# A hybrid decoder layer on one core: smaller groups for z, another product order, conv means two tiles sooner, all low weights on VectorE

## The chip, the core and the metric

The kernel runs on one core of a Trainium2 chip. A core has a matrix engine (TensorE, PE in the profile; its weight loads are PEld), VectorE (DVE), ScalarE (ACT), GpSimd (POOL) and SyncE (SP), which here issues most of the DMA transfers. The metric is the device time of one launch in microseconds (us). Three runs of the kernel before took 1290.45, 1290.51 and 1292.22 us.

## The reference

One layer of a decoder, for 1024 tokens of width 1024, with 16 meta tokens put in front (1040 rows). All is in 32-bit floats.

- `h` is the layer norm of the input. `z = h @ w_in + b_in` is cut into queries (512 columns), keys (128), values (128), the input of a convolution branch (2 x 512) and gates (2 x 1024).
- Attention branch: 8 query heads on 2 key heads of width 64, a window of 128 positions in blocks of 128, 16 meta keys that are always seen, a relative bias and a sink in the softmax. Its output is projected to width 1024.
- Convolution branch: `c = value * sigmoid(gate)`, a causal depthwise convolution over 31 taps, a layer norm over the 512 channels, `silu`, a projection to width 1024.
- `mixed = sigmoid(g_A) * A + sigmoid(g_B) * B`, then `h = LN(alpha * h + mixed @ w_out)`.
- A feed-forward part: up to 2 x 2816 columns, a causal depthwise convolution over 3 taps, `gelu(g) * u`, down to 1024, and a last layer norm.

## The kernel before

**Products.** Activations are kept transposed: channels on the partitions, rows (tokens) along the free axis. A tile of 128 output channels is one set of weights, 8 blocks of 128 x 128 for a depth of 1024. To keep the precision of 32-bit floats, each operand is split into a high half, rounded to TensorE's 32-bit format, and a low half, the rest. `product` (lines 334, 337 and 338) then issues three matmuls for each block: high weights by high activations, high by low, low by high. So each weight tile needs `split` (line 300: ScalarE copies and rounds the high half; line 303: the low half by a subtraction, on VectorE if `quick`, else on POOL). `weights` counts the tiles; the first thirty are quick, and the last eight of them, those of the two projections, are not. `prep_wo` splits the eight weight tiles of the output product with the same function: the first four on VectorE, the last four on POOL.

**z.** `z_tile` takes one weight tile through a list of groups of columns; each group is accumulated over 8 blocks x 3 matmuls into one bank of PSUM (tag "mm", three banks) and evicted. HG, the list for the convolution tiles, has 272, 384 and 384 columns; TG, the list for queries and gates, is the same without the first 14 rows (258, 384, 384). There are 27 such tiles: 8 of the convolution (`conv_chunk`, a gate tile and a value tile for each of four chunks), 3 of queries and 16 of gates (`gate_tile`; line 716 evicts a gate through a Tanh on ScalarE, and the result is stored to DRAM as `sgd`). The first products of z (line 540) run earlier, while the input is still being normalised.

**Order.** The program is written in one sequence with priorities (`rank`, `tc.cur_priority`); a scheduler orders each engine's instructions by them when the kernel is built, and the engines run their queues in that order. `after` adds an edge for that scheduler alone. Attention (lines 780 to 900) has a higher priority than the gate tiles, and the 124 operations of the 31 taps of four chunks (lines 707 and 709, VectorE) a lower one, so gate tiles fill TensorE and taps fill VectorE between the steps of attention. A step there is: scores (lines 870 and 871, TensorE), bias and maximum (line 874, VectorE), exponentials (line 886, ScalarE), transposes (line 894), splits of the weights (line 897 ScalarE, line 898 VectorE) and the product with the values.

**The norm of the convolution branch.** `csum` adds the four chunks (POOL twice, then VectorE, line 925). The means (line 930) are products of `csum` with a matrix of 1/512, held back until gate tile 12. Then come, for three groups of columns (UG: 386, 384, 256), the centring (line 968), squares and their sum (974 to 980), the inverse root with a refinement step (985 to 989: one table function on ScalarE, four operations on VectorE), the scaling and Silu (996, 997), and the split (1003, 1004). ScalarE's functions lie in tables; the profile shows an ACT_TABLE_LOAD where another table is needed. VectorE's operations there are pinned in the written order. `o_split` (1015 to 1017) divides attention's output by the softmax sums and splits it. These are the operands of the two projections (`ps_p`), eight weight tiles in groups PG of 258 and 3 x 256 columns.

**The feed-forward part.** The up-projection (`prod`, line 1509) is done in seven products in place of eight, on sums of halves: for each of 22 pairs of output chunks, seven products of 24 matmuls each, 12 on 258 and 12 on 256 columns. The seven operands of both halves of the rows lie where B_AT says, in the buffers RHC, RHO, OA, RX and OC. The weights come from a ring (RING) which takes over the buffers of the earlier weight tiles. The down-projection is line 1634.

**Places.** High and low halves of a weight tile are two buffers, "whi" and "wlo", of 8 blocks of 144 columns each, of which 128 are used. W_FLAT = 96 is where a flat row of 1024 begins in one of them.

Of the kernel before, what the change touches and what calls it, by code (L numbers as in the profile page):

```python
# [29 lines left out]
P = 128  # L30
# [22 lines left out]
HG = [(0, 272), (272, 656), (656, 1040)]  # L53
UG = [(0, 386), (386, 770), (770, 1026)]
# [15 lines left out]
W_FLAT = 96  # L70
# [40 lines left out]
def tile_hybrid_layer(  # L111
# [187 lines left out]
    def split(raw, hi, lo, quick=False, behind=None):  # L299
        ins = nc.scalar.copy(hi, raw)  # L300
        if behind is not None:
            after(ins, behind)
        return (nc.vector if quick else nc.gpsimd).tensor_tensor(lo, raw, f32(hi), OP.subtract)  # L303
# [26 lines left out]
    def product(ps, terms, behind=None):  # L330

        n = len(terms)
        for i, (ah, al, bh, bl) in enumerate(terms):
            ins = nc.tensor.matmul(ps, ah, bh, start=i == 0, stop=False)  # L334
            if i == 0 and behind is not None:
                after(ins, behind)
            nc.tensor.matmul(ps, ah, bl, start=False, stop=False)  # L337
            last = nc.tensor.matmul(ps, al, bh, start=False, stop=i == n - 1)  # L338
# [16 lines left out]

    TG = [(a + U0 if i == 0 else a, b) for i, (a, b) in enumerate(HG)]

# [168 lines left out]
    def z_first(g, tiles, *ks, raw=False):  # L526
# [5 lines left out]
        for k in ks:  # L532
            for i in tiles:
# [5 lines left out]
                for j, (w, hl) in enumerate(((hi, 0), (hi, 1), (lo, 0))):  # L539
# [122 lines left out]
    ones = ones_of(cp)  # L662
# [22 lines left out]
    def conv_chunk(c):  # L685
# [8 lines left out]
        z_tile(in_cols(10 + c), HG, g_evac, wt_c1 if c == 1 else None)  # L694
# [7 lines left out]
        z_tile(in_cols(6 + c), HG, v_evac2)  # L702
        with rank(RK_CONV + c * 100):
            for j in range(TAPS):
                wc = cdw[:, j * CH + c:j * CH + c + 1]
                if j == 0:
                    nc.vector.tensor_scalar(acc[c], cin[:, j:j + U], wc, cdwb(c), OP.mult, OP.add)
                else:
# [1079 lines left out]
```

## Time and profile before

| what | value |
|---|---|
| median of three runs | 1290.51 us |
| the profiled execution, its own time | 1288.89 us |
| its span, first to last instruction | 1287.0 us |
| mean granted TensorE clock | 0.994 |
| TensorE busy | 1263.6 us |
| VectorE busy | 1083.7 us |
| ScalarE busy | 582.9 us |
| POOL busy | 49.8 us |

A rough course of the time, from the windows and the timeline: to 60 us the input norm and the first products of z, from then to 433 us the tiles of z with attention and the taps between them, to 520 us the two projections, to 631 us the output product and its norm, from about 639 to 1068 us the up-projection, then the down-projection and the last norm.

How to read the rows: times are in us from the first instruction. A row of the timeline has the start, the length, the engine, the line, the operation, the output and input by their names, the shape and a count; brackets behind it give the time that the engine had idled before it and what released it. The length of a matmul includes its way through the array, so consecutive matmuls overlap; the pace is the distance between their starts. A row of a group ends in busy time and mean length (us, ns), and then the idle time before its instructions and what ended it. A row of the windows has the window and its length, then busy time and count for each engine, the granted clock, the share of DMA time and GB/s. A row of the chain of waits has the start, the length, the engine, the output and the line.

### The profile page before, as it was taken

The numbers are of one execution on the slowest core, as the hardware profiler recorded it, in microseconds if no ns is written. First come the engines' busy times: TensorE is split into PE (matmuls) and PEld (weight loads), VectorE is DVE, ScalarE is ACT, GpSimd is POOL, SyncE is SP. The second block draws the span as 40 slices with busy tenths as digits, with TensorE's granted clock in tenths as the row PEclk, the third lists the DMA queues.
The fourth block names the chain that finished last, engine by engine and source line by source line (L and its number), as shares of the span: only waits on it lengthen the run. The fifth ranks groups of instructions, "written<-read, shape, count | busy, mean of one in ns | idle before, by whom it ended". The sixth has DMA issues, their size and how long they took to land.

```text
span 1287.0 us, 21685 instructions
## 1 busy us (share of the span) xinstructions
PE 1263.6 (98%) x8546; PEld 1191.0 (93%) x8546; DVE 1083.7 (84%) x1843; ACT 582.9 (45%) x1053; POOL 49.8 (4%) x28
## 2 busy tenths in 40 slices
PE   8999999999999999999999999999999999999997
PEld 7899999999999999788899999999999997888886
DVE  7889999999936987647899999989889886887697
ACT  5423334545547232244664554455545543535330
POOL 2100000010000132100000000000000000000000
PEclk8999999999999999999999999999999999999999
DMA  6265633333252665222235554453454566989722
GB/s 246 83 241 165 163 108 98 89 99 107 76 150 64 188 189 143 89 82 90 76 117 196 184 202 177 180 210 130 161 187 187 189 209 244 393 291 381 254 76 82
DMA packets 96296, 212.10 MB, mean 165 GB/s; under 512 B 11059, under 2 KB 36211, under 8 KB 95938
## 3 DMA queue, kind: packets, MB, share of 16 engines
q1 hardware_dynamic: 84426, 199.64, 46.3%
q10 hardware_dynamic: 11768, 11.08, 2.7%
q8 instruction: 67, 1.10, 0.4%
q14 instruction: 35, 0.29, 0.1%
HBM read 150.29 MB, written 62.70 MB: 165 GB/s over the span
## 4 chain that ended last, share of the span: by engine, by line
PE 88%; DVE 6%; DMA 2%; ACT 2%; issue 1%; SPq 0%; POOL 0%; DVEq 0%; ACTq 0%
PE px L1509 14%; PE py L1509 9%; PE ps_x L1634 9%; PE ps_z L334 7%; PE ps_z L337 7%; PE ps_z L338 7%; PE ps_z L1634 5%; PE pz L1509 5%; PE pw L1509 5%; PE ps_w L338 2%; PE ps_w L334 2%; PE ps_w L337 2%; PE ps_p L338 2%; PE ps_p L334 2%; PE ps_p L337 2%; DVE RHC L509 1%
## 5 line engine op out<-in xcount | busy, mean ns | idle before, releaser
L334 PE MATMUL ps_z<-RHO,whi 128*128 128x384 f32 (+2 forms) x648 | 210.9, 326 | 2.0 <-ACT FA L716 2.0
L337 PE MATMUL ps_z<-RHC,whi 128*128 128x384 f32 (+2 forms) x648 | 210.1, 324 | 0.0
L338 PE MATMUL ps_z<-RHO,wlo 128*128 128x384 f32 (+2 forms) x648 | 208.6, 322 | 0.0
L709 DVE SCALAR_TENSOR_TENSOR FA<-cin,cdw,FA 128x1026 f32<-128x1026 f32 x120 | 153.2, 1291 | 0.2
L334 PEld LDWEIGHTS ps_z<-RHO,whi 128*128 128x128 f32 x648 | 122.2, 189 | 3.5 <-ACT FA L716 2.3
L337 PEld LDWEIGHTS ps_z<-RHC,whi 128*128 128x128 f32 x648 | 122.4, 189 | 0.8
L338 PEld LDWEIGHTS ps_z<-RHO,wlo 128*128 128x128 f32 x648 | 122.1, 189 | 0.9 <-issue 0.3
L300 ACT CAST whi<-wr 128x1024 fp32r<-128x1024 f32 x37 | 38.8, 1047 | 83.2 <-PE ps_z L337 67.9
L1331 DVE TENSOR_TENSOR RHO<-wr,RHO 128x512 fp32r<-128x512 f32 x94 | 63.4, 684 | 9.8 <-ACT RHO L1330 9.8
L1330 ACT CAST RHO<-wr 128x512 fp32r<-128x512 f32 x94 | 56.6, 619 | 22.2 <-DVE wr L1348 9.9
L1348 DVE TENSOR_TENSOR wr<-wr 128x512 f32<-128x512 f32 x88 | 60.1, 683 | 0.2
L1521 ACT COPY FA<-px 128x514 f32<-128x514 f32 (+2 forms) x23 | 13.1, 571 | 81.5 <-PE px L1509 81.5
L716 ACT ACTIVATE FA<-ps_z,colr 128x384 f32<-128x384 f32 (+1 forms) x48 | 26.1, 543 | 45.9 <-PE ps_z L338 41.6
L303 DVE TENSOR_TENSOR wlo<-wr,whi 128x1024 fp32r<-128x1024 f32 x27 | 32.8, 1216 | 14.5 <-ACT whi L300 14.4
L1509 PE MATMUL px<-OA,RHO 128*128 128x258 f32 x324 | 43.2, 282 | 0.0
L1436 ACT ACTIVATE FA<-OB,coll 128x512 f32<-128x512 f32 x44 | 35.9, 815 | 14.8 <-DVE OB L1517 14.7
L1509 PE MATMUL px<-OC,RHO 128*128 128x256 f32 x324 | 42.2, 280 | 0.0
L1521 ACT COPY OB<-px 128x514 f32<-128x514 f32 (+2 forms) x46 | 26.1, 568 | 35.3 <-PE px L1509 35.2
L1509 PE MATMUL px<-RHC,RHO 128*128 128x258 f32 (+1 forms) x312 | 41.0, 280 | 0.5 <-ACT OB L1521 0.5
L1509 PEld LDWEIGHTS px<-OA,RHO 128*128 128x128 f32 x324 | 40.5, 189 | 0.2 <-ACT OB L1521 0.2
L1509 PEld LDWEIGHTS px<-OC,RHO 128*128 128x128 f32 x324 | 39.9, 189 | 0.1
L1509 PEld LDWEIGHTS px<-RHC,RHO 128*128 128x128 f32 x312 | 38.5, 189 | 0.7 <-ACT OB L1521 0.7
(468 smaller groups left out, 3374.4 us busy)
## 6 DMA issues: line engine op xcount, KB each, us to landing
wr<-in_w_up_dram SPq DMA_DIRECT2D x44, 512.0 KB, 4.1
wr<-in_w_z_dram SPq DMA_DIRECT2D x29, 512.0 KB, 3.8
fd<-FA SPq DMA_DIRECT2D x44, 256.0 KB, 2.4
OB<-in_w_down_dram SPq DMA_DIRECT2D x21, 512.0 KB, 3.9
FA<-sd SPq DMA_DIRECT2D x15, 512.0 KB, 9.1
qt<-qd SPq DMA_DIRECT2D x28, 256.0 KB, 4.1
sgd<-FA ACTq DMA_DIRECT2D x32, 192.0 KB, 2.6
td<-OB SPq DMA_DIRECT2D x12, 512.0 KB, 3.6
```

Of the source, the lines that this page charges most:

```text
L300: ins = nc.scalar.copy(hi, raw)
L334: ins = nc.tensor.matmul(ps, ah, bh, start=i == 0, stop=False)
L337: nc.tensor.matmul(ps, ah, bl, start=False, stop=False)
L338: last = nc.tensor.matmul(ps, al, bh, start=False, stop=i == n - 1)
L709: nc.vector.scalar_tensor_tensor(acc[c], cin[:, j:j + U], wc, acc[c], OP.mult, OP.add)
L1330: nc.scalar.copy(hi, src)
L1331: ins = nc.vector.tensor_tensor(lo, src, f32(hi), OP.subtract)
L1348: ins = nc.vector.tensor_tensor(*x)
L1436: nc.scalar.activation(t, cc[:, 2:HW], AF.Identity, bias=ffw(3, o), scale=ffw(2, o))
L1509: ins = nc.tensor.matmul(o, x[:, ks], bmat(sub, q, hl, k), start=first and k + j == 0, stop=k == 3 and j == 2, skip_group_check=not first)
L1521: copied.append(nc.scalar.copy(*x))
L1634: nc.tensor.matmul(banks[i], l[:, ts], r[:, ws], start=first and a and x + k == 0, stop=z and x == len(ops) - 1 and k == 2, skip_group_che ...
```

## The change

- HG is joined by ZG (272 and 3 x 256 columns), which now serves `conv_chunk` and TG. A tile of z has 96 matmuls instead of 72; the columns are the same.
- `product` issues low weights by high activations first, then high by high, then high by low. The same order is used in the first products of z. The up- and down-projections keep theirs.
- The two halves of a weight tile lie in one buffer "w", at the offsets W_AT (0 and 1136 elements) or, flat, at W_FLAT (96 and 1248).
- `split` makes every low half on VectorE. That concerns the eight weight tiles of the projections and four of the output product.
- The three operands of the up-projection in RHC, RHO and RX (first half of the rows) move by 40, 40 and 56 elements.
- The means wait for gate tile 10 instead of 12. The norm is written in another order: all centrings, all sums of squares, roots 0 and 1, scaling 0, root 2, scalings 1 and 2, then the splits; the Silu operations of scaling 0 are put behind root 2. The sums of squares use two tags of PSUM in turn.
- The bias loads are written first, then the convolution tiles of chunk 1, then the meta values, the keys, constants and zeroed buffers (held behind the meta values), then the tiles of chunk 0, then the values (their transposes held behind the third group of the gate tile of chunk 0), then the taps of both chunks. `conv_chunk` returns the function that writes the taps.

```diff
 HG = [(0, 272), (272, 656), (656, 1040)]
+ZG = [(0, 272), (272, 528), (528, 784), (784, 1040)]
 UG = [(0, 386), (386, 770), (770, 1026)]
...
 RX_WO = 16
-W_FLAT = 96
+W_AT = (0, 1136)
+W_FLAT = (96, 1136 + 112)
 R_DN = 112
...
 
-    def ones_of(pool):
+    def ones_of(pool, behind=None):
         t = pool.tile([P, P], F, name="ones", tag="ones", bufs=1)
-        nc.vector.memset(t, 1.0 / CW)
+        ins = nc.vector.memset(t, 1.0 / CW)
+        if behind is not None:
+            after(ins, behind)
         return t
...
 
-    def split(raw, hi, lo, quick=False, behind=None):
+    def split(raw, hi, lo, behind=None):
         ins = nc.scalar.copy(hi, raw)
...
             after(ins, behind)
-        return (nc.vector if quick else nc.gpsimd).tensor_tensor(lo, raw, f32(hi), OP.subtract)
+        return nc.vector.tensor_tensor(lo, raw, f32(hi), OP.subtract)
+
+    def chunks(t):
+        return [t[:, o:o + KC * WS].rearrange("p (k c) -> p k c", k=KC)[:, :, :P] for o in W_AT]
 
-    def wsp(tag, dtype=R):
-        return wsp_p.tile([P, KC, WS], dtype, name=tag, tag=tag)
+    def wsp(dtype=R):
+        return wsp_p.tile([P, 2 * KC * WS], dtype, name="w", tag="w")
 
-    def wsp_flat(tag, dtype=R):
-        return wsp(tag, dtype).rearrange("p k c -> p (k c)")[:, W_FLAT:W_FLAT + D]
+    def wsp_flat(dtype=R):
+        t = wsp(dtype)
+        return [t[:, o:o + D] for o in W_FLAT]
 
-    fills, cin_done, gate_mm = [0], [], {}
+    fills, cin_done, gate_mm, gate_last = [0], [], {}, []
     last_fill, last_split = [], []
...
             last_fill.append(fill(raw))
-        hi, lo = ((sp.tile([P, KC, WS], R, name=t + "3") if own else wsp(t))[:, :, :P] for t in ("whi", "wlo"))
+        hi, lo = chunks(sp.tile([P, 2 * KC * WS], R, name="w3") if own else wsp())
         if n <= 3:
...
         with rank(RK_SPLIT):
-            last_split.append(split(raw, hi, lo, n <= 30))
+            last_split.append(split(raw, hi, lo))
             if n == 7:
...
         for i, (ah, al, bh, bl) in enumerate(terms):
-            ins = nc.tensor.matmul(ps, ah, bh, start=i == 0, stop=False)
+            ins = nc.tensor.matmul(ps, al, bh, start=i == 0, stop=False)
             if i == 0 and behind is not None:
                 after(ins, behind)
-            nc.tensor.matmul(ps, ah, bl, start=False, stop=False)
-            last = nc.tensor.matmul(ps, al, bh, start=False, stop=i == n - 1)
+            nc.tensor.matmul(ps, ah, bh, start=False, stop=False)
+            last = nc.tensor.matmul(ps, ah, bl, start=False, stop=i == n - 1)
         return last
...
 
-    TG = [(a + U0 if i == 0 else a, b) for i, (a, b) in enumerate(HG)]
+    TG = [(a + U0 if i == 0 else a, b) for i, (a, b) in enumerate(ZG)]
 
...
                     continue
-                for j, (w, hl) in enumerate(((hi, 0), (hi, 1), (lo, 0))):
+                for j, (w, hl) in enumerate(((lo, 0), (hi, 0), (hi, 1))):
                     ins = nc.tensor.matmul(sums0[i], w[:, k], h0(k, hl, a, b), start=k + j == 0,
...
     cp = att.enter_context(tc.tile_pool(name="cin", bufs=2, side="right", reuse_waits="tile"))
-    ones = ones_of(cp)
     cdw = cp.tile([P, TAPS * CH], F, name="cdw", tag="cdw", bufs=1)
...
     vm = ap.tile([P, NKV, 2, HD], R, name="vm")
-    nc.vector.memset(f32(vm[64:]), 0.0)
     pmTs = [ap.tile([P, 512], R, name=f"pmT{i}") for i in range(2)]
-    for t in pmTs:
-        nc.vector.memset(f32(t[64:]), 0.0)
     bias = ap.tile([P, NH, 272], F, name="bias")
...
 
-        z_tile(in_cols(10 + c), HG, g_evac, wt_c1 if c == 1 else None)
+        gate_last.append(z_tile(in_cols(10 + c), ZG, g_evac, wt_c1 if c == 1 else None))
         cin = cp.tile([P, 16 + T], F, name="cin", tag="cin")
...
 
-        z_tile(in_cols(6 + c), HG, v_evac2)
-        with rank(RK_CONV + c * 100):
...
+        z_tile(in_cols(6 + c), ZG, v_evac2)
+
+        def taps():
+            with rank(RK_CONV + c * 100):
+                for j in range(TAPS):
+                    wc = cdw[:, j * CH + c:j * CH + c + 1]
+                    if j == 0:
+                        nc.vector.tensor_scalar(acc[c], cin[:, j:j + U], wc, cdwb(c), OP.mult, OP.add)
+                    else:
+                        nc.vector.scalar_tensor_tensor(acc[c], cin[:, j:j + U], wc, acc[c], OP.mult, OP.add)
+
+        return taps
 
...
 
-    for g in range(NKV):
...
     tc.cur_priority = RK_QKV + 2000
...
 
+    tc.cur_priority = RK_QKV + 4000
+    taps = [conv_chunk(1)]
+    cin4 = cin_done[-1]
     vmT = ap.tile([P, 64], F, name="vmT")
-    nc.vector.memset(vmT, 0.0)
+    after(nc.vector.memset(vmT, 0.0), cin4)
     for hl in range(2):
         for g in range(NKV):
-            nc.vector.tensor_copy(vmT[g * HD:(g + 1) * HD, hl * 32 + g * 16:hl * 32 + g * 16 + 16],
+            vm_ins = nc.vector.tensor_copy(vmT[g * HD:(g + 1) * HD, hl * 32 + g * 16:hl * 32 + g * 16 + 16],
                                   vT[g * HD:(g + 1) * HD, 0:16])
+    tc.cur_priority = RK_QKV + 1000
+    for g in range(NKV):
+        kr = FA[:, 2054 + g * T:2054 + (g + 1) * T]
+        for h in range(2):
+            load(kr[h * HD:(h + 1) * HD, :T], kd[g * HD:(g + 1) * HD, :])
+        for lo in (0, 64):
+            for o, i in ((Kx[g][lo:, :, 16:144], kr[lo:, 16:T].rearrange("p (n c) -> p n c", c=P)),
+                         (Kx[g][lo:, :, 0:16], kr[lo:, 0:16].unsqueeze(1).to_broadcast([P - lo, NB, 16]))):
+                if lo == 0:
+                    ins = nc.vector.tensor_copy(o, i)
+                else:
+                    ins = nc.vector.tensor_tensor(o, i, f32(o), OP.subtract)
+                after(ins, vm_ins)
+    ones = ones_of(cp, vm_ins)
+    for t in [vm] + pmTs:
+        after(nc.vector.memset(f32(t[64:]), 0.0), vm_ins)
+    tc.cur_priority = RK_QKV + 4000
+    taps.append(conv_chunk(0))
+    tc.cur_priority = RK_QKV + 2000
     ps = pat.tile([P, 512], F, name="ps_vm", tag="t", bufs=2)
-    nc.tensor.transpose(ps[:64, :P], vmT, ident)
+    after(nc.tensor.transpose(ps[:64, :P], vmT, ident), gate_last[-1][2])
     src = ps[:64, :P].rearrange("p (g d) -> p g d", d=HD)
...
             c = NMETA + (q4 * 4 + i) * P
-            nc.tensor.transpose(ps[:, i * P:(i + 1) * P], vT[:, c:c + P], ident)
+            after(nc.tensor.transpose(ps[:, i * P:(i + 1) * P], vT[:, c:c + P], ident), gate_last[-1][2])
         src = ps[:, :].rearrange("p (n g d) -> p n g d", g=2, d=HD)
...
             nc.vector.tensor_tensor(lo, src[:, :, g, :], f32(hi), OP.subtract)
-
-    tc.cur_priority = RK_QKV + 4000
-    conv_chunk(1)
-    conv_chunk(0)
+    for t in taps:
+        t()
+    tc.cur_priority = RK_QKV + 5000
     for r in range(1, 4):
...
     pm = ap.tile([P, 4, 64], F, name="pm", tag="pm", bufs=2)
-    nc.vector.memset(pm, 0.0)
+    after(nc.vector.memset(pm, 0.0), cin_done[-1])
     for g in range(NKV):
...
         if isinstance(o, str):
-            conv_chunk(int(o[1]))
+            conv_chunk(int(o[1]))()
         else:
...
             ins = nc.tensor.matmul(means[g][:, :b - a], ones, csum[:, a:b], start=True, stop=True)
-            after(ins, gate_mm[12][0])
+            after(ins, gate_mm[10][0])
     att.close()
...
     dve = nc.vector
-    sums, rstd = {}, {}
+    sums, rstd, roots, silus = {}, {}, [], []
 
...
             pin(dve.tensor_tensor(s_, s_, q_, OP.add))
-        sums[g] = pat.tile([P, 512], F, name="ps_m", tag="s", bufs=2)
+        sums[g] = pat.tile([P, 512], F, name="ps_m", tag="st"[g % 2], bufs=2)
         nc.tensor.matmul(sums[g][:, :n], ones, s_, start=True, stop=True)
...
         pv_, r_, t_ = sums[g][:, :n], temp(n), temp(n)
-        nc.scalar.activation(r_, pv_, AF.Abs_reciprocal_sqrt, bias=eps, scale=1.0)
+        roots.append(nc.scalar.activation(r_, pv_, AF.Abs_reciprocal_sqrt, bias=eps, scale=1.0))
         pin(dve.scalar_tensor_tensor(t_, pv_, EPS, r_, OP.add, OP.mult))
...
             pin(dve.tensor_tensor(y, y, rstd[g], OP.mult))
-            nc.scalar.activation(y, y, AF.Silu, bias=clnb(c), scale=clng(c))
+            silus.append(nc.scalar.activation(y, y, AF.Silu, bias=clnb(c), scale=clng(c)))
 
...
     tc.cur_priority = RK_CLN
-    cln_centre(0)
-    cln_centre(1)
-    cln_var(0)
-    cln_centre(2)
-    cln_var(1)
+    for g in range(3):
+        cln_centre(g)
+    for g in range(3):
+        cln_var(g)
     cln_rstd(0)
-    cln_scale(0)
-    cln_var(2)
     cln_rstd(1)
-    cln_scale(1)
-    cln_split(0)
+    cln_scale(0)
     cln_rstd(2)
+    for ins in silus:
+        after(ins, roots[2])
+    cln_scale(1)
     cln_scale(2)
+    cln_split(0)
     cln_split(1)
...
         else:
-            hi, lo = (wsp_flat(n) for n in ("whi", "wlo"))
+            hi, lo = wsp_flat()
         if raw is None:
...
             load(raw, w_out_v[k])
-        split(raw, hi, lo, k < 4, behind)
+        split(raw, hi, lo, behind)
         wo[k] = (hi, lo)
...
 
-    B_AT = [[(RHC, 0), (RHO, 4096)] + [(OA, OA_UP + i * KC * BS[0]) for i in range(4)] + [(RX, 0)],
+    B_AT = [[(RHC, 40), (RHO, 4096 + 40)] + [(OA, OA_UP + i * KC * BS[0]) for i in range(4)] + [(RX, 56)],
             [(OC, OC_UP + i * 2048) for i in range(4)] + [(RHC, 4096 + R_DN), (RHC, 2048 + R_DN), (RHC, 6144 + R_DN)]]
...
         if RING[i] is None:
-            RING[i] = wsp_flat(("whi", "wlo")[i % 2])
+            RING[i:i + 2] = wsp_flat()
         t = RING[i]
```

More of the change, by code (lines that the diff above doesn't have):

```diff
@@ L700, in v_evac2 @@
                                                            OP.add, OP.mult))
-        z_tile(in_cols(6 + c), HG, v_evac2)
-        with rank(RK_CONV + c * 100):
[L704 to L708, printed above, removed]
-                    nc.vector.scalar_tensor_tensor(acc[c], cin[:, j:j + U], wc, acc[c], OP.mult, OP.add)
+        z_tile(in_cols(6 + c), ZG, v_evac2)
[8 more added lines that the diff above has]
+        return taps
     def gate_tile(i):
@@ L1092, in tile_hybrid_layer @@
     GS += [(OB, i * 516) for i in range(5)]
-    W_AT = (2064, 3088, 0, 1024)
+    E_AT = (2064, 3088, 0, 1024)
     def gslot():
@@ L1656, in ln_rows @@
     def ln_rows():
-        return [wsp_flat(t, F) for t in ("whi", "wlo")]
+        return wsp_flat(F)
     gains = ln_rows()
```

28 lines of the change are left out of this document (13 added, 15 removed).

## The prediction

> **What bounds the kernel now.** I read the busy shares first, then the stalls of TensorE, then its pace group by group, then the stages by window. The page's first part and its largest group:
>
> ```profile
> PE 1263.6 (98%) x8546; PEld 1191.0 (93%) x8546; DVE 1083.7 (84%) x1843; ACT 582.9 (45%) x1053; POOL 49.8 (4%) x28
> L334 PE MATMUL ps_z<-RHO,whi 128*128 128x384 f32 (+2 forms) x648 | 210.9, 326 | 2.0 <-ACT FA L716 2.0
> ```
>
> TensorE is busy for 98% of 1287.0 us, so an edit can gain in two ways only: fewer nanoseconds per matmul, or fewer of the few waits. "Busy" does not say at what pace. The pace is the distance between starts, read in the timeline of TensorE: where a gate tile of z begins (258 columns), where its 384-column groups begin, where the next tile begins; then the same for two tiles of the projections, which already use 258 + 3 x 256.
>
> ```profile
> 122.27 0.28 PE L334 MATMUL ps_z<-RHO,whi 128*128 128x258 f32 x1
> 125.14 0.34 PE L334 MATMUL ps_z<-RHO,whi 128*128 128x384 f32 x1
> 133.71 0.28 PE L334 MATMUL ps_z<-RHO,whi 128*128 128x258 f32 x1
> ...
> 479.75 0.28 PE L334 MATMUL ps_p<-OA,whi 128*128 128x258 f32 x1
> 482.64 0.28 PE L334 MATMUL ps_p<-OA,whi 128*128 128x256 f32 x1
> 491.06 0.28 PE L334 MATMUL ps_p<-OA,whi 128*128 128x258 f32 x1
> ```
>
> The gate tile takes 11.44 us: 24 matmuls of 258 in 2.87 (119.6 ns each), 48 of 384 in 8.57 (178.5 each). The projection tile has the same 1026 columns in 96 matmuls and takes 11.31: 24 of 258 in 2.89, 72 of 256 in 8.42 (116.9 each). So more and smaller groups are not dearer here. The up-projection shows that 256 columns have two paces:
>
> ```profile
> 852.04 1.58 PE L1509 MATMUL pz<-OC,RHO 128*128 128x256 f32 x12
> 853.46 1.59 PE L1509 MATMUL px<-OA,RHO 128*128 128x258 f32 x12
> ...
> 860.53 1.53 PE L1509 MATMUL py<-OC,RHO 128*128 128x256 f32 x12
> 861.90 1.36 PE L1509 MATMUL px<-OA,RHO 128*128 128x258 f32 x10
> ```
>
> Twelve matmuls of pz take 1.42 us (118.3 ns each), twelve of py 1.37 (114.2), with nothing waiting. What differs is which buffers feed them. The chain of waits shows it as a fixed pattern, group by group:
>
> ```profile
> 847.92 2.85 PE px L1509 x24
> 850.77 2.85 PE pz L1509 x24
> 853.62 2.81 PE px L1509 x24
> ...
> 864.87 2.86 PE py L1509 x24
> 867.73 2.85 PE px L1509 x24
> ```
>
> One round of seven products (24 matmuls each) lasts 19.81 us (847.92 to 867.73); three take 2.85, 2.85 and 2.86, four take 2.81. The three are those whose first operand is kept in RHC, RHO and RX; in the code these start at other distances from a multiple of 256 bytes than the other four.
>
> Then the waits. In 385 to 437 us TensorE waits twice for long; the rows show it, with what ScalarE and VectorE were doing:
>
> ```profile
> 414.11 0.45 PE L334 MATMUL ps_z<-RHO,whi 128*128 128x384 f32 x1 [2.01 <-ACT FA L716]
> 435.49 0.39 PE L337 MATMUL ps_p<-OA,whi 128*128 128x258 f32 x1 [1.90 <-DVE OA L1017]
> ```
> ```profile
> 393.23 1.28 ACT L985 ACT_TABLE_LOAD   x1
> ...
> 405.26 0.58 ACT L716 ACTIVATE FA<-ps_z,colr 128x384 f32<-128x384 f32 x1
> ...
> 410.04 1.28 ACT L997 ACT_TABLE_LOAD   x1
> ...
> 413.49 0.57 ACT L716 ACTIVATE FA<-ps_z,colr 128x384 f32<-128x384 f32 x1
> ```
> ```profile
> 421.73 2.56 DVE L1003 CAST OC<-FA 128x384 fp32r<-128x384 f32 x1
> ...
> 431.37 0.56 DVE L1017 TENSOR_TENSOR OA<-OB,OA 128x386 fp32r<-128x386 f32 x1
> ...
> 432.83 2.61 DVE L1017 TENSOR_TENSOR OA<-OB,OA 128x386 fp32r<-128x386 f32 x1
> ```
> ```profile
> 421.34 2.73 POOL L303 TENSOR_TENSOR wlo<-wr,whi 128x1024 fp32r<-128x1024 f32 x1 [129.15 <-ACT whi L300]
> 432.54 2.47 POOL L303 TENSOR_TENSOR wlo<-wr,whi 128x1024 fp32r<-128x1024 f32 x1 [8.47 <-ACT whi L300]
> ```
>
> First wait: ScalarE reloads its table eight times from 393.23 to 410.04 (L985, L716 and L997 in turn) and evicts no gate group between 405.26 and 413.49. Second wait: the last low half before the first projection takes 2.61 us, while POOL splits weights beside it. Where VectorE has room, by windows:
>
> ```profile
> core 0: us, PE busy (x) PEld busy (x) DVE busy (x) ACT busy (x) POOL busy (x), PEclk, DMA share, GB/s
> 157.50:339.20 181.70, 181.70 (x1196) 178.20 (x1196) 175.75 (x358) 85.74 (x226) 6.23 (x2) 1.00 0.36 100
> 352.00:385.00 33.00, 33.00 (x205) 31.49 (x205) 12.35 (x26) 14.30 (x32) 0.00 (x0) 1.00 0.50 147
> 412.00:436.00 24.00, 20.10 (x118) 19.79 (x118) 21.63 (x42) 9.68 (x17) 5.21 (x2) 0.93 0.64 184
> 436.00:520.00 84.00, 83.89 (x711) 83.69 (x710) 68.42 (x147) 22.98 (x47) 21.99 (x9) 1.00 0.60 164
> ```
>
> In the attention stage VectorE is 97% busy beside a full TensorE; right after it, 37%.
>
> **The change part by part.** *Groups of z.* 27 tiles go from 72 to 96 matmuls with the same columns. The first group stays; 72 of 256 replace 48 of 384. At 114.2 ns these are 8.22 us, at 116.9 8.42, at 118.3 8.52, against 8.57: a tile gains 0.35, 0.15 or 0.05 us, all 27 gain 9.5, 4.1 or 1.4. Which pace holds depends on addresses. Before, high and low weights lie at the same remainder, and the distance from the moving operand to the next weights changes from product to product. Afterwards one buffer holds both at remainders that differ by 64 bytes, and with the product order low-high, high-high, high-low that distance is the same for every matmul. The groups of 256 that run at 114.2 are also fed from addresses that repeat with a steady distance, so I take 114.2; the row it is nearest to otherwise is the projections' 116.9. The price on ScalarE: a fourth, smaller eviction and one more store per tile; ScalarE is 45% busy, which hides it.
>
> The Trainium skill, "TensorE: Matmul & The Clock Gate", section "Wait — 56ns, not 53.3ns?", speaks against smaller groups: each matmul costs its columns plus a fixed 2.5 ns or so, whatever its length. By it the 648 added matmuls would cost an estimated 1.6 us instead of gaining 9.5. The rows disagree: 96 matmuls took 11.31 us where 72 took 11.44 for the same columns.
>
> *Projections* (L1110 and after) have their groups of 256 already; with the new order they go from 116.9 to 114.2: 72 x 2.7 ns x 8 tiles = 1.6 us less (0 if the pace stays).
>
> *Starts of three up-projection operands.* The offsets 40, 40 and 56 give them the remainder of the four fast ones. 2.85 + 2.85 + 2.86 - 3 x 2.81 = 0.13 us a round, 22 rounds (44 chunks, two at a time): 2.9 less. No instruction is added. Bounds: 0 to 2.9; I take 2.9, since the same line already runs both ways.
>
> *Conv means two tiles sooner, roots adjacent.* The rows of the sums and the means:
>
> ```profile
> 350.38 1.20 DVE L925 TENSOR_TENSOR csum<-csum,FA 128x1026 f32<-128x1026 f32 x1
> 381.58 1.67 PE L930 MATMUL ps_m<-csum,ones 128*128 128x386 f32 x5
> ```
>
> The means start 30.0 us after their operand is there. Two tiles sooner takes 22.9 off that, so the norm's chain has 22.9 us more before the projections need it, and the 1.90 wait goes. Roots 0 and 1 adjacent and the first Silu behind root 2 leave five table loads of eight: 3 x 1.28 = 3.8 us less on ScalarE in that stretch, more than the 2.01 wait. Against it, three banks of 256 cover 72 x 114.2 = 8.2 us of late evictions, where banks of 384 cover 72 x 178.5 = 12.9; so this wait lies between gone and another 2.0. I take both as gone: 3.9 less.
>
> *Low weights on VectorE.* Twelve subtractions leave POOL (2.47 to 2.73 us each in the rows above). On VectorE one takes:
>
> ```profile
> L303 DVE TENSOR_TENSOR wlo<-wr,whi 128x1024 fp32r<-128x1024 f32 x26 | 31.6, 1215 | 11.7 <-ACT whi L300 11.6
> ```
>
> 12 x 1.215 = 14.6 us. VectorE has 15.6 us free in 436 to 520, and it gets back the stretch of the operations beside POOL: L1017 takes 0.56 us at 431.37 against 2.61 at 432.83. Between 14.6 and a small gain I take 0, hidden by TensorE's work in that window. If that cover were gone, each late weight tile would cost its 1.2 us.
>
> *Values, keys, memsets and taps in a new order.* The conv tile of chunk 1 goes ahead of the key and value splits; the six bias loads go on SP's queue ahead of its weights. The TensorE order of the changed program starts attention at the same column count (282 thousand) and ends it after 666 thousand columns instead of 739 thousand. So VectorE, at 97%, must deliver attention's work within fewer columns, and the means, 22.9 us sooner and after some 17 faster tiles (6 us), arrive at about 352.7 against csum's end at 351.6. TensorE's queue is in order: a late softmax or csum holds every gate matmul behind it. The trace has no such wait. Lower bound 0; upper bound: the step that turns probabilities into weights shows with its whole length at each of 30 units,
>
> ```profile
> L886 ACT ACTIVATE s<-s,sm 128x272 f32<-128x272 f32 (+1 forms) x64 | 31.8, 500 | 9.6 <-DVE sm L882 9.1 <-DVE sm L883 0.4
> L898 DVE TENSOR_TENSOR pl<-ps_t,ph 128x512 fp32r<-128x512 f32 x30 | 20.5, 685 | 4.7 <-ACT ph L897 4.5
> ```
>
> 0.500 + 0.685 = 1.19 us each, 36 us. VectorE's 6 us of idle time in that stage is the nearest measure of how far TensorE can run ahead; most of it stays covered, and I take 4.
>
> *Sum.* -9.5 - 1.6 - 2.9 - 3.9 + 4 = -13.9. The profiled execution has 1288.89 us (span 1287.0), so 1275.0; it stands 1.6 under the median of 1290.51, so 1276.6, said as 1277.
>
> **The rivals.**
> First, the z and projection groups stay at the pace that 256 columns have in the projections now, 116.9: the distance is not what counts. For it: the rows at 479.75. Then -4.1 + 0 - 2.9 - 3.9 + 4 = -6.9, 1283.6.
>
> Second, a matmul has a fixed price and the pace of 384 columns was only a buffer's accident, so that z gets 1.6 us dearer: +1.6 - 2.9 - 3.9 + 4 = -1.2, 1289.3, no change that can be told. Against it: the two tiles above. (It is the rule of the page cited.)
>
> Third, on the other side: VectorE becomes the bound of attention. TensorE meets softmax and transposes earlier in its queue than VectorE delivers them, and each unit shows its 1.19 us. For it: 97%. Against it: attention starts where it did, and the taps can give way. All gains of 17.9 are used up when 15 of 30 units show; at 20 units it is -17.9 + 23.8 = +5.9, 1296.4.
>
> **How the numbers follow.** Forecast 0.44; first rival 0.26; second 0.12; third 0.18. 0.2% is 2.6 us, about what a measurement of this kernel can tell from no change. Faster: 0.44 + 0.26 and 0.02 of the second, 0.72; same 0.10; slower 0.18. The forecast's own range is 1270 (no wait in attention, and stalls of under 1 us elsewhere going too) to 1282. The range 1270 to 1293 leaves out most of the third case (0.14) and 0.05 below.
>
> **What the profile of the changed kernel would show.** Pace: a gate tile of 96 matmuls in 11.1 us if right, 11.3 by the first rival, over 11.5 by the second. Up-projection: the chain's seven products all at 2.81, a round in 19.7. Norm: five table loads behind the means, no TensorE wait on L716 or L1017; the means at 353 to 359. POOL: no L303 row, and no VectorE row of 2.5 us in 412 to 520. Attention: idle time of TensorE put down to L898, L882 or the csum line; 4 us in sum if right, over 18 if the third rival holds. The prediction is wrong if the first operand of the projections comes later than the last gate matmul, or if the tile's pace does not move and attention waits too.

## The result

| | median of five runs (lowest to highest), us | ratio to before (95% interval) |
|---|---|---|
| before | 1290.51 (1288.61 to 1292.22) | 1 |
| changed | 1284.68 (1284.34 to 1285.99) | 0.9957 (0.9943 to 0.9972) |

The kernel became 0.43% faster, some 5.8 us. Forecast were 13.5 us and a range from 1270 to 1293: the sign was right and the size was not.

The profiled execution of the changed kernel took 1284.34 us with a span of 1282.6, against 1288.89 and 1287.0. Where the span's 4.4 us lie, from the first matmul of each kind in the timelines:

| stretch | before | changed | difference |
|---|---|---|---|
| start to the first gate tile | 62.9 | 64.5 | +1.6 |
| tiles of z with attention, up to the first projection | 368.4 | 369.3 | +0.9 |
| projections, output product, to the up-projection | 195.1 | 191.4 | -3.7 |
| up-projection | 439.1 | 436.9 | -2.2 |
| the rest | 221.4 | 220.5 | -0.9 |

The first row is scatter: it lay between 62.0 and 65.4 us in all the profiled executions shown here, the kernel before among them. The stage that was to gain most, z, gained nothing in sum.

**Pace.** The timeline of TensorE in the changed kernel, a gate tile of 96 matmuls from its first start, over that of its 256-column groups, to the next tile:

```profile
123.60 0.28 PE L342 MATMUL ps_z<-RHO,w 128*128 128x258 f32 x1
126.47 0.28 PE L342 MATMUL ps_z<-RHO,w 128*128 128x256 f32 x1
134.79 0.28 PE L342 MATMUL ps_z<-RHO,w 128*128 128x258 f32 x1
```

11.19 us where the tile shown of before took 11.44; 72 matmuls of 256 take 8.32, 115.6 ns each. The pace within the tile is not even. Each block of 128 rows of the weights takes three matmuls, and the first matmul of each block in the third group starts at:

```profile
129.27 0.28 PE L342 MATMUL ps_z<-RHO,w 128*128 128x256 f32 x1
129.61 0.28 PE L342 MATMUL ps_z<-RHO,w 128*128 128x256 f32 x1
129.96 0.28 PE L342 MATMUL ps_z<-RHO,w 128*128 128x256 f32 x1
130.30 0.28 PE L342 MATMUL ps_z<-RHO,w 128*128 128x256 f32 x1
```

One block takes 0.34 us, the next 0.35, and so on in turn; to the nanosecond 340 and 350, or 113.3 and 116.7 a matmul.

**Norm.** Table loads of ScalarE between 352 and 440 us, grouped by line, are five, where the same view of before has eight:

```profile
L1002 ACT ACT_TABLE_LOAD x2 | 2.6, 1283 | 0.5 <-DVE t L1003 0.4
L724 ACT ACT_TABLE_LOAD x2 | 2.6, 1283 | 0.0
L1014 ACT ACT_TABLE_LOAD x1 | 1.3, 1283 | 0.4 <-DVE t L1003 0.4
```

The view of waits has all that TensorE waited for between 62 and 440 us, first in the kernel before, then in the changed one:

```profile
PE ps_z L334 <- ACT FA L716: 2.0, 1, 2.0
PE ps_p L337 <- DVE OA L1017: 1.9, 1, 1.9
```
```profile
PE ps_s L887 <- DVE sm L891: 2.8, 2, 2.3
PE ps_t L911 <- ACT pmT L834: 0.7, 1, 0.7
PE ps_pm L831 <- DVE pl L915: 0.2, 1, 0.2
```

Both old waits are gone. A new one has come, in attention. The windows around it (same columns as in the prediction) and the two longest waits in the timeline:

```profile
194.00:196.00 2.00, 0.00 (x0) 0.00 (x0) 2.00 (x7) 0.46 (x1) 0.00 (x0) 1.00 0.00 0
196.00:198.00 2.00, 1.48 (x9) 1.14 (x9) 1.97 (x7) 0.20 (x1) 0.00 (x0) 1.00 0.00 0
198.00:200.00 2.00, 1.57 (x7) 1.40 (x8) 1.97 (x4) 0.95 (x3) 0.00 (x0) 0.57 0.86 217
200.00:202.00 2.00, 1.50 (x7) 1.10 (x6) 2.00 (x9) 0.17 (x1) 0.00 (x0) 0.50 0.21 45
202.00:204.00 2.00, 2.00 (x11) 2.00 (x11) 1.87 (x6) 0.00 (x0) 0.00 (x0) 0.50 0.00 0
204.00:206.00 2.00, 2.00 (x14) 2.00 (x14) 2.00 (x7) 1.20 (x5) 0.00 (x0) 0.73 0.00 0
```
```profile
196.10 0.39 PE L887 MATMUL ps_s<-kx,qt 128*128 128x272 f32 x1 [2.27 <-DVE sm L891]
...
198.43 2.01 PE L911 MATMUL ps_t<-coll,s 128*128 128x128 f32 x8 [0.66 <-ACT pmT L834]
```

From 194 to 196 us TensorE does nothing while VectorE is full. The waits of the list add up to 3.7 us, but more is lost: from 198 to 206 us the granted clock is mostly at a half, also where TensorE is fully busy again. Summed over all starts between 185 and 225 us, the matmuls take 10.7 us more than their columns need at 226.7 ns for 512, against 3.1 in the kernel before: 7.6 us lost.

**Up-projection.** Its chain of waits, one round:

```profile
668.54 2.81 PE px L1526 x24
671.35 2.81 PE pz L1526 x24
674.17 2.81 PE px L1526 x24
...
685.42 2.81 PE py L1526 x24
688.23 2.81 PE px L1526 x24
```

All seven products take 2.81; a round takes 19.69 us instead of 19.81.

### The profile page after: what moved, and what is told of

It reads as the page before. It is cut to its first block, busy times and chain, and to the rows that moved or that the text cites. A ratio compares the mean times of both kernels' runs of the same rounds, so it can differ in the third digit from the quotient of the medians.

```text
span 1282.6 us, 23049 instructions
## 1 busy us (share of the span) xinstructions
PE 1260.1 (98%) x9194; PEld 1187.8 (93%) x9194; DVE 1076.1 (84%) x1862; ACT 586.0 (46%) x1080; POOL 18.6 (1%) x16
## 4 chain that ended last, share of the span: by engine, by line
PE 92%; DVE 5%; DMA 1%; issue 1%; ACT 1%; SPq 0%; POOL 0%; DVEq 0%; ACTq 0%
PE px L1526 14%; PE py L1526 9%; PE ps_x L1651 9%; PE ps_z L342 8%; PE ps_z L346 8%; PE ps_z L345 8%; PE ps_z L1651 5%; PE pz L1526 5%; PE pw L1526 5%; PE ps_p L346 2%; PE ps_p L342 2%; PE ps_p L345 2%; PE ps_w L346 2%; PE ps_w L342 2%; PE ps_w L345 2%; PE ps_z L548 1%
## 5 line engine op out<-in xcount | busy, mean ns | idle before, releaser
L346 PE MATMUL ps_z<-RHC,w 128*128 128x256 f32 (+2 forms) x864 | 244.5, 283 | 0.0
L342 PE MATMUL ps_z<-RHO,w 128*128 128x256 f32 (+2 forms) x864 | 244.5, 283 | 0.0
L345 PE MATMUL ps_z<-RHO,w 128*128 128x256 f32 (+2 forms) x864 | 243.8, 282 | 0.0
L342 PEld LDWEIGHTS ps_z<-RHO,w 128*128 128x128 f32 x864 | 163.2, 189 | 0.9 <-issue 0.3
L346 PEld LDWEIGHTS ps_z<-RHC,w 128*128 128x128 f32 x864 | 163.4, 189 | 0.6
L345 PEld LDWEIGHTS ps_z<-RHO,w 128*128 128x128 f32 x864 | 163.3, 189 | 0.4
L307 DVE TENSOR_TENSOR w<-wr,w 128x1024 fp32r<-128x1024 f32 x37 | 45.1, 1219 | 26.8 <-ACT w L304 26.7
L304 ACT CAST w<-wr 128x1024 fp32r<-128x1024 f32 x37 | 38.8, 1047 | 54.7 <-PE ps_z L346 36.4
L724 ACT ACTIVATE FA<-ps_z,colr 128x258 f32<-128x258 f32 (+1 forms) x64 | 30.1, 471 | 58.9 <-PE ps_z L346 48.3
L1348 DVE TENSOR_TENSOR w<-wr,w 128x512 fp32r<-128x512 f32 x60 | 40.7, 688 | 4.9 <-ACT w L1347 4.7
L1347 ACT CAST w<-wr 128x512 fp32r<-128x512 f32 x60 | 36.3, 618 | 12.8 <-DVE wr L1365 6.4
```

Source lines behind the costliest of these rows:

```text
L307: return nc.vector.tensor_tensor(lo, raw, f32(hi), OP.subtract)
L342: ins = nc.tensor.matmul(ps, al, bh, start=i == 0, stop=False)
L345: nc.tensor.matmul(ps, ah, bh, start=False, stop=False)
L346: last = nc.tensor.matmul(ps, ah, bl, start=False, stop=i == n - 1)
L1347: nc.scalar.copy(hi, src)
L1348: ins = nc.vector.tensor_tensor(lo, src, f32(hi), OP.subtract)
```

## The experiments

Where did the wait at 193 us come from? VectorE's timeline in the changed kernel, just after the first convolution tiles:

```profile
89.91 0.07 DVE L700 MEMSET cin<- 128x16 f32 x1 [3.58 <-DMA v1d<-vrow]
94.49 0.48 DVE L703 SCALAR_TENSOR_TENSOR cin<-ps_z,colr,FA 128x256 f32<-128x256 f32 x1 [4.51 <-PE ps_z L346]
...
105.80 0.82 DVE L713 TENSOR_SCALAR FA<-cin,cdw,colr 128x1026 f32<-128x1026 f32 x1 [0.24 <-PE ps_v L774]
```

VectorE idles for 8.1 us between 86 and 95 us, in two stretches, since the key splits and the zeroing, which filled this time before, are held behind the meta values, and these behind the convolution tile. The first tap is at 105.80; before it was at 101.28. **Theory A**: this missing time comes back at 193 us, when attention's steps stand in VectorE's queue behind taps that are late. **Rival B**: attention simply lies too dense in TensorE's queue. Each run below was measured against the kernel before on the same chip.

### The keys not held back

```diff
-    after(nc.vector.memset(vmT, 0.0), cin4)
+    nc.vector.memset(vmT, 0.0)
...
-                after(ins, vm_ins)
-    ones = ones_of(cp, vm_ins)
+    ones = ones_of(cp)
...
-        after(nc.vector.memset(f32(t[64:]), 0.0), vm_ins)
+        nc.vector.memset(f32(t[64:]), 0.0)
...
-    after(nc.vector.memset(pm, 0.0), cin_done[-1])
+    nc.vector.memset(pm, 0.0)
```

> The changed kernel, but the key splits, the constant and the zeroed buffers are not held behind the meta values. Theory A (the TensorE wait and the low clock at 193 to 206 us come from VectorE work that was put off: VectorE idles for 8 us between 86 and 95 us, and that time is missing when attention's steps queue behind taps): VectorE fills the hole, the first tap starts 3 to 5 us sooner, the wait of 2.27 us and the clock of 0.5 behind it go, 5 to 7 us faster than the changed kernel, ratio 0.990 to 0.992. Rival B (attention lies too dense in TensorE's queue for VectorE at 97 to 99%, wherever the keys are split): the wait stays or moves later, ratio 0.995 to 0.997.

Measured: 1283.64 us, 0.9950 (0.9938 to 0.9961), hardly better than the changed kernel. The wait at 193 us is gone, as A says; but two others have come, and the timelines of TensorE and ScalarE name their source:

```profile
97.53 0.52 PE L342 MATMUL ps_z<-RHO,w 128*128 128x256 f32 x1 [3.30 <-ACT FA L695]
108.08 0.39 PE L342 MATMUL ps_z<-RHO,w 128*128 128x272 f32 x1 [1.71 <-DVE w L307]
```
```profile
96.99 0.49 ACT L695 ACTIVATE FA<-ps_z,colr 128x272 f32<-128x272 f32 x1 [18.70 <-DVE kx L757]
```

ScalarE's eviction of a gate group waits for the last key split. The code says why: the keys lie in FA up to element 4134, the eviction slots begin at 4104. Thirty columns overlap. The ratio is the one that B expected, not A's, and A missed a second point: VectorE's hole was not filled. It idles for 4.04, 4.99 and 1.63 us between 86 and 107 us, and its first tap comes at 107.95, some 2 us later than in the changed kernel instead of 3 to 5 sooner. TensorE is late as well, by 7.1 us at attention's first scores (164.3 instead of 157.2). So this run alone does not show that filling the hole cures the wait.

### And the overlap taken away

```diff
-    def stage(n, lo=4104, cnt=5):
+    def stage(n, lo=4136, cnt=5):
```

> The changed kernel with nothing held behind the meta values, as in the run before, and with the slots into which ScalarE evicts gate groups moved from element 4104 of FA to 4136, so that they no longer overlap the last 30 columns of the keys. Theory A (the two new waits of 3.46 and 1.87 us at 97 and 108 us came from ScalarE's line 695, which had to wait for VectorE's last key split because of that overlap): both go, the wait at 193 us stays away, about 5 us faster than the run with the keys unheld, ratio 0.990 to 0.992. Rival B (VectorE is short of time in attention in any case): the wait comes back near 193 to 206 us, ratio 0.994 to 0.996.

Measured: 1278.39 us, 0.9906 (0.9890 to 0.9921). Theory A holds, but for one wait that stays. The waits of TensorE between 62 and 440 us, and the windows around 194 us:

```profile
PE ps_z L342 <- DVE w L307: 1.7, 1, 1.7
```
```profile
186.00:194.00 8.00, 8.00 (x71) 7.99 (x69) 8.00 (x20) 3.13 (x16) 0.00 (x0) 1.00 0.50 131
194.00:206.00 12.00, 12.00 (x104) 11.79 (x102) 11.88 (x32) 6.25 (x20) 0.00 (x0) 1.00 0.36 99
```

One wait of 1.7 us is left (at 102 us, not at 108); the expectation had it gone too. The time beyond the columns' need between 185 and 225 us, the excess, is 3.4 us, near the 3.1 of before, with attention's products just as dense (scores from 158.2 to 326.7 us; 157.2 to 324.4 in the changed kernel, 156.6 to 351.7 before). This version beats both kernels.

### The overlap alone

The slots at 4136, all holds kept.

> The changed kernel with the eviction slots moved from 4104 to 4136 alone, keys and zeroed buffers still held behind the meta values. Theory A (it is the hold that leaves VectorE idle at 86 to 95 us, and the missing time that stops TensorE at 193 us): idle time and wait stay, ratio 0.995 to 0.997. Rival B (the overlap alone is at fault): the wait goes, ratio 0.990 to 0.992.

Measured: 1294.51 us, 1.0033 (1.0021 to 1.0044): slower than the kernel before, which neither side had expected. The planner now put the value tile of chunk 1 later, and VectorE's hole grew:

```profile
87.26 0.07 DVE L700 MEMSET cin<- 128x16 f32 x1 [2.51 <-DMA v1d<-vrow]
98.46 0.48 DVE L703 SCALAR_TENSOR_TENSOR cin<-ps_z,colr,FA 128x256 f32<-128x256 f32 x1 [11.13 <-PE ps_z L346]
```
```profile
200.00:250.00 50.00, 46.62 (x319) 43.37 (x320) 48.83 (x116) 26.28 (x73) 0.00 (x0) 0.86 0.35 93
```

The hole is 13.6 us instead of 8.1, the excess between 185 and 225 us 17.2 instead of 10.7, the mean clock from 200 to 250 us 0.86. The profiled span is 10.0 us longer than the changed kernel's: 6.5 are this excess, and some 3.8 a wait of TensorE of 2.1 us at 100 us with the clock at a half for 3.4 us behind it. Against the changed kernel the loss in attention grows with the hole a hundred microseconds earlier, which speaks for A's cause, though A's ratio was missed.

### The old order of preparation, without and with the overlap

The block of preparation as in the kernel before, the rest as changed; then the same with the slots at 4136.

> The changed kernel with values, keys, constants and taps prepared in the order of the kernel before. Theory A (the new preparation order causes the wait and the low clock at 193 to 206 us): the wait goes, 4 to 7 us faster than the changed kernel, ratio 0.990 to 0.993. Rival B (the faster tiles of z let TensorE run into VectorE in attention, whatever was prepared first): a wait of 1 to 3 us with a low clock stays in 190 to 300 us, ratio 0.995 to 0.997.

Measured: 1283.47 us, 0.9945 (0.9933 to 0.9958). The ratio lies between the two that were expected. No wait is left at 193 us, but one at 97.9 us that no theory had named; waits of TensorE, and ScalarE's row:

```profile
PE ps_vm L760 <- DVE vmT L757: 5.1, 1, 5.1
```
```profile
96.90 0.49 ACT L699 ACTIVATE FA<-ps_z,colr 128x272 f32<-128x272 f32 x1 [6.80 <-DVE kx L743]
```

> The changed kernel with the preparation order of the kernel before and the eviction slots moved from element 4104 to 4136 of FA. Theory A (in the old order the wait of 5.1 us at 97.9 us has the same root, ScalarE's line 699 behind the last key split because the slot overlaps the keys): the wait goes and none takes its place, ratio 0.990 to 0.992, so that the order of preparation itself is worth nothing once the overlap is gone. Rival B (the transposes of the values come too early in TensorE's queue in the old order): a wait at 92 to 98 us stays, ratio 0.993 to 0.995.

Measured: 1278.80 us, 0.9908 (0.9895 to 0.9922). The wait shrank to 2.5 us and did not go, so B has a part in it, but the time is that of the best version (0.9906). The new order of preparation is therefore worth nothing by itself. By the ratios the old order lost 4.8 us to the overlap, and the new one 6.6 us to holds and overlap together; taking only the holds from the new one gained 0.9 us, taking only the overlap cost 9.8.

### Groups and addresses of z

Groups of z as before:

```diff
-ZG = [(0, 272), (272, 528), (528, 784), (784, 1040)]
+ZG = [(0, 272), (272, 656), (656, 1040)]
```

> The changed kernel with the groups of z as before (272, 384, 384), all else changed. Theory A (a group of 256 runs at 115.9 ns a matmul and one of 384 at 176.4, so 72 of the one save 0.12 us a tile against 48 of the other): 27 tiles, 3.2 us slower than the changed kernel, part of it hidden because TensorE then meets VectorE's late softmax at 193 us some 1.5 us less early; ratio 0.997 to 0.998. Rival B, the prediction's 0.35 us a tile: 9.5 us slower than the changed kernel, ratio 1.003. Rival C, a fixed price per matmul: 1.6 us faster than the changed kernel, ratio 0.994.

Old product order and equal remainders of both halves (W_AT = (0, 1152), W_FLAT = (96, 1248) with product lines as before):

> The changed kernel with the product order of before (high-high, high-low, low-high) and the low half of a weight tile at the same remainder as the high half (1152 elements behind it instead of 1136). Theory A (addresses and order set the pace of the groups of 256): z and projections go from 115.9 and 115.6 ns back to about 117.5, 27 + 8 tiles of 72 matmuls at 1.6 to 1.9 ns, 4.2 us slower than the changed kernel, ratio 0.999. Rival B (256 columns are faster whatever the order): the pace stays under 116, ratio 0.996.

Equal remainders alone, and the old product order alone:

> The changed kernel with the low half of a weight tile at the same remainder as the high half, the new product order kept. One look, for the pace of the 256-column groups of z alone, which was 115.9 ns with both and 117.6 with neither. Theory A (a steady distance between moving operand and weights needs both): 117 to 118. Rival B (the order alone does it): 115.9.

> The changed kernel with the product order of before, the new places of the weights kept. One look, for the same pace. Theory A (both are needed): 117 to 118. Rival B (the places alone do it): 115.9.

| version | us | ratio | undisturbed gate tile, us | mean of all 256- (or 384-) column matmuls of z, ns |
|---|---|---|---|---|
| before | 1290.51 | 1 | 11.44 | (176.4) |
| changed | 1284.68 | 0.9957 | 11.19 | 115.9 |
| old groups | 1287.31 | 0.9977 (0.9968 to 0.9986) | 11.31 | (176.1) |
| old order and old places | 1287.81 | 0.9983 (0.9974 to 0.9992) | 11.31 | 117.6 |
| old places | 1286.96, one run | | 11.31 | 117.6 |
| old order | 1289.21, one run | | 11.38 | 118.2 |

A tile of the version with old groups, to be read against the tile of the changed kernel above:

```profile
121.54 0.28 PE L342 MATMUL ps_z<-RHO,w 128*128 128x258 f32 x1
124.39 0.34 PE L342 MATMUL ps_z<-RHO,w 128*128 128x384 f32 x1
132.84 0.28 PE L342 MATMUL ps_z<-RHO,w 128*128 128x258 f32 x1
```

A's paces are met in the first three; in the fourth 118.2 lies just above its 117 to 118, on A's side. Groups of 256 are worth 0.12 us a tile at the new addresses (11.31 to 11.19). The ratios differ by 2.6 us (0.0020), but not from the pace alone: in the profiled execution with old groups attention lost 1.3 us more (an excess of 12.0 instead of 10.7). At the old addresses groups of 256 are worth nothing: 1944 matmuls at 117.6, with the 258- and 272-column ones, take 307.4 us by their means, and so do those of the kernel before. For the pace of the 256-column matmuls the new places and the new order work only together; the new places without the order run slowest of all.

### Offsets of the up-projection

```diff
-    B_AT = [[(RHC, 0), (RHO, 4096)] + ... + [(RX, 0)],
+    B_AT = [[(RHC, 40), (RHO, 4096 + 40)] + ... + [(RX, 56)],
```

> The kernel before with one part of the change alone: the three operands of the up-projection in RHC, RHO and RX moved by 40, 40 and 56 elements. Theory A (the start of these operands sets the pace of the three slow products of each round): all seven products of a round take 2.81 us, the up-projection is 2.1 to 2.9 us shorter, ratio 0.998, and nothing else moves. Rival B (the pace in the changed kernel came from where the weights lie in their buffer, not from these operands): 2.85, 2.85 and 2.86 stay, ratio 1.000.

Measured: 1289.12 us, 0.9991 (0.9983 to 1.0000). In its profile the up-projection takes 436.3 us instead of 439.1, and all seven products 2.81: the cause is A. The medians show only 1.2 us of the 2.8. One thing that differed is the clock: the mean granted clock of the eleven executions was 0.9932, that of the 28 of the kernel before 0.9940, which would make some 1.0 us (an estimate: 0.0008 of the span). In the profiled execution the stretch from the first projection to the up-projection took 198.5 us instead of 195.1, and the clock stood at a half for 6.8 us behind the wait at the first projection, which is 2.1 us long here and 1.9 before. The first two windows of it:

```profile
436.00:438.00 2.00, 1.54 (x7) 1.54 (x8) 1.93 (x5) 0.00 (x0) 0.00 (x0) 0.50 0.57 224
438.00:440.00 2.00, 2.00 (x11) 2.00 (x11) 1.90 (x5) 0.00 (x0) 0.00 (x0) 0.50 0.01 5
```

### The norm and the low weights

The means behind gate tile 12 and the old order of the norm, in the changed kernel:

> The changed kernel with the means behind gate tile 12 again and the norm in its old order (a root, a scaling, a Silu in turn, eight table loads for five). Theory A (the two waits of 2.01 and 1.90 us before were caused by these): TensorE waits again on the gate eviction, 2 to 4 us since three banks of 256 cover 8.3 us instead of 12.7, and at the first projection, 0 to 2 us; ratio 0.998 to 1.000. Rival B (the low weights on VectorE alone had removed the stretch that made the norm late): no wait, ratio 0.9955 to 0.9965.

Measured: 1286.30 us, 0.9972 (0.9960 to 0.9984), 1.9 us slower than the changed kernel by the ratios. Its waits of TensorE:

```profile
PE ps_z L342 <- ACT FA L724: 2.8, 2, 2.0
PE ps_s L887 <- DVE sm L891: 2.4, 1, 2.4
PE ps_t L911 <- ACT pmT L834: 0.7, 1, 0.7
```

The wait on gate evictions is back, the one at the first projection is not; the ratio, between the two that were expected, does not tell the theories apart. The twelve low weights back on POOL, with the new norm:

> The changed kernel with the twelve low weights of before on POOL again. Theory A (with the norm some 20 us earlier nothing waits for VectorE there any more, and the stretch of single operations to 2.6 us beside POOL is hidden): as the changed kernel within 0.1%, ratio 0.9950 to 0.9965, with rows of 2.5 us on VectorE and no wait of TensorE. Rival B (the move was needed): a TensorE wait of 1 to 2 us on line 1034 or on a low weight, ratio 0.997.

Measured: 1284.35 us, 0.9952 (0.9940 to 0.9965), as the changed kernel, with POOL's rows of 2.4 to 2.6 us back and no TensorE wait near the projections. So the wait at the projection went by either of the two edits: the earlier norm removes it, and so does the work taken from POOL.

## Why the prediction was right in sign and wrong in size

*The pace of z: the term was mis-sized, -9.5 forecast, -3.3 measured* (means of all matmuls of z of 256, 258, 272 and 384 columns: 307.4 us before, 304.1 changed). The step that failed is the choice of two rows as representative. The tile taken for before (11.44 us, 178.5 ns for 384 columns) stands for the gate tiles that nothing interrupts (11.43 to 11.44), but the convolution tiles and those among attention's products run faster; the mean of all 1296 was 176.4. That is 2.7 us of the gap. And the fast row of the up-projection, 114.2 ns, was taken for the new groups, since the distance between weights and moving operand would be the same for every matmul; they reached 115.9 on the mean, 3.3 us more. Half of the mechanism holds: places and product order set the pace together, and the undoing of either took the gain away. The other half does not: by the offsets in the code that distance, as a remainder of 256 bytes, is the same in every block, yet in the tile shown only every second block reaches 113.3 ns, and the others take 116.7. The remainder of the starts moves on by 64 bytes from one block to the next; whether that is the reason was not tried. The first rival's price (116.9, -4.1) was nearer. That its time, 1283.6, is so near to the measured one is luck: its terms for attention and norm were as wrong as the forecast's, and its reason, that these groups stay at the pace of the projections before, is refuted, for the projections' own pace moved too.

*Projections, -1.6:* 117.4 to 115.6 ns for 576 matmuls, -1.0.

*Offsets, -2.9:* -2.2 in the changed kernel, -2.8 alone.

*Norm, -3.9:* both waits went, and five table loads for eight, as forecast; -5.7 measured. Its price was too small by what follows a wait. In the kernel before, the tile with the first wait lasts from 404.79 to 419.96 us, 15.17 instead of 11.44: 3.7 us for a wait of 2.01, and the windows behind it show why:

```profile
414.00:416.00 2.00, 1.89 (x7) 1.89 (x8) 1.97 (x4) 1.54 (x4) 0.00 (x0) 0.68 0.59 119
416.00:418.00 2.00, 2.00 (x8) 2.00 (x8) 1.86 (x6) 0.06 (x1) 0.00 (x0) 0.50 0.72 212
```

With the second wait, 5.6 to 5.8 us went, as this one execution has it. The means came at 366.0, not at 353 to 359, since attention was late (359.8 in the version at 0.9906); with `csum` ready at 357.5 nothing waited for them.

*Low weights, 0:* right.

*Preparation and dense attention, +4: mis-sized, +7.6 measured, and its cause was not the one given.* I looked at how densely attention lies in the queues; the two runs at 0.991 have it as dense and lose nothing there. The loss comes with VectorE's hole at 86 to 95 us. I had costed the holds behind the meta values at nothing and had not asked what VectorE does while it waits. The third rival named the right engine and the right place, with too large a price (23.8). That the clock would fall was in no step.

The hole alone is not the measure, as the version with the keys not held shows, which has one of 10.7 us and loses nothing here. What orders all fourteen profiled executions is how many taps VectorE has done when attention's first scores start. Windows from 60 us to that moment give the busy time and number of all taps but the first (lines 709 and 715), in the kernel before, the changed one, the one with the keys not held, and the one with the overlap alone taken away:

```profile
60.00:156.58 96.58, 41.22 (x34) 1.00 0.64 192
60.00:157.17 97.17, 38.05 (x31) 1.00 0.68 197
60.00:164.30 104.30, 41.30 (x34) 0.98 0.61 180
60.00:159.10 99.10, 34.21 (x28) 0.98 0.64 180
```

With the first tap these are 35, 32, 35 and 29. The six executions with 35 or 38 have an excess of 2.9 to 3.4 us between 185 and 225 us, the seven with 31 to 33 one of 9.0 to 12.0, the one with 29 17.2. No run changed this number alone, so it is an order seen in the traces and not a tested cause.

*The rest.* -3.3 - 1.0 - 2.2 - 5.7 + 7.6 = -4.6, and +1.6 from the start makes -3.0 of the measured -4.4. About 0.9 of what is left lies behind the up-projection. There most versions built on the changed kernel are 0.6 to 1.0 us shorter and two are 0.2 longer, so it may be scatter; it stays open.

## What to carry to other kernels

- Take a pace from the mean of all instructions of its kind, never from one tile: where addresses set the pace, one tile is a sample of one.
- When an edit holds work back on an engine that is nearly full later, look for the idle time it leaves now, and for how far that engine still leads the one that will wait for it: here the time came back as a wait of TensorE 100 us later. Where work cannot be pulled into the hole, look for two buffers that overlap by a few columns.
- Price a TensorE wait of 2 us at up to twice its length, since the granted clock may fall behind it; the same wait can pass without that in another execution.

## What the runs showed of the hardware

- The clock fell to a half behind waits of 2.3 us (in attention) and of 2.0 us (before, at 414), but not behind those of 1.9 us (before, at 435) and of 2.0 us (old norm). With the offsets alone it was the other way about: it fell behind the wait of 2.1 us at 436, not behind that of 2.0 us at 417. With the old groups it fell at 198.6 us and stayed low for 10.2 us, though no wait before that was longer than 0.91 us. It stayed low for 6.8 us in the first case (from the windows: 0.57, 0.50, 0.50 and 0.73 over 2 us each) and for about 3.4 in the second. The Trainium skill, "TensorE: Matmul & The Clock Gate", section "What's actually happening", gives a free-running window of 3.4 us after which activity is judged; the lengths agree with two windows and one, and with three for the old groups. That an idle window is needed does not agree as stated: the waits of 0.91 to 2.3 us before these falls were shorter than a window.
- Matmuls of the same shape with nothing waiting run at 113.6 to 118.3 ns for 256 columns, 4% apart, by the places of the operands and the order of the products, and even one tile holds blocks at 113.3 and at 116.7. More and shorter matmuls cost nothing by themselves: at the old places and order, all of z takes 307.4 us with groups of 256 as with groups of 384.
